# Attention scores: the two banks' products with the key's low half, 64 array rows each

## The chip, the cores and the metric

The kernel runs on one core of one Trainium2 chip. The metric is the device time of one execution in microseconds. The core has a matrix engine (TensorE, PE in the profile; its weight loads are listed as PEld), three engines for elementwise work (VectorE or DVE, ScalarE or ACT, GpSimd or POOL), and a synchronisation engine (SyncE, SP) that mostly issues DMA transfers. Each engine runs its own instructions in order and waits for the others through semaphores. The array of the matrix engine has 128 rows, along which a product is summed, and 128 columns; a stationary operand ("weights") is loaded into it, and a moving operand of up to 512 columns streams past. Results go to PSUM, in banks of 512 fp32 values for each of 128 partitions.

## The reference

One layer of a hybrid encoder is computed for a prompt of 1024 tokens and a decode sample of 32 tokens. The part that matters is the attention of the prompt over 8 heads of 64 values. An indexer has chosen 256 keys for each query; the others are masked out:

```python
s = jnp.einsum('bthd,btkhd->bthk', q.astype(f32), kg) * (HEAD_DIM ** -0.5)
s = jnp.where(valid[:, :, None, :], s, -jnp.inf)
p = jax.nn.softmax(s, axis=-1)
return jnp.einsum('bthk,btkhd->bthd', p, vg)
```

Queries of one chunk of 64 tokens see the keys up to the end of their chunk, so a tile of 128 queries, number i of 0 to 7, needs the first 128 (i + 1) keys. The kernel computes the scores of all these keys and adds a mask.

## The kernel before

Most products are made in a reduced fp32 format (`F32R`), in which one operand is split into a high half H and a low half L = x - H, and several products are added up in PSUM to win back the lost digits. The large projections do it with three (`mm3`, lines 272 to 274).

**Scores.** A head has only 64 values, half the rows of the array. The kernel uses the other half for the low part of the query: for head e of a pair (e is 0 or 1), `X.qs[e]` is a tile of 128 partitions, with the query's high half in the partitions 64e to 64e + 63 and its low half in the other 64. The key is stored twice, in both halves of the partitions of `X.kH[e]` (high) and `X.kL[e]` (low). A single product of `qs` with `kH` so gives q_high k_high + q_low k_high, and one of `qs` with `kL` adds q_high k_low + q_low k_low. `Soft.products` (line 1410) does these two products for each PSUM bank (line 1420): tiles with up to 512 keys have one bank, larger ones two banks of 320, 384, 448 or 512 columns (i = 4, 5, 6, 7). The order is kH, kL for the first bank, then kH, kL for the second.

**Order of the work.** Attention runs over four pairs of heads, p = 0 to 3, and in each over both heads and eight query tiles; these items stand in one list (`seq`). The loop at line 1730 takes one step for each item k: the scores of item k on TensorE; its row maxima on DVE, which read the PSUM banks (line 1426); the output product of item k - 3 (line 1530); the transposes of item k - 2 (line 1513), whose results ACT and DVE copy (1515, 1516); the exponentials of item k on ACT (line 1433), and normalisations (1440, 1442). Between these, `run(...)` deals in pieces of the large projections (the stream `Z`, `pz` in the profile), written out by hand so that TensorE has other work while the elementwise engines turn one tile's scores into weights. The pair p = 3 goes through its query tiles as i = 6, 7, 4, 5, 2, 3, 0, 1, the others from 0 to 7. An item of another kind (`Sample`, once in each pair) handles the 32 decode queries with plain fp32 operands; its transposes (line 1476) have only 64 rows, and one of its products (line 1485, tile `vts`) only 32.

`begin()` (line 1448) runs once for each pair, ahead of the scores of its first item; it loads the gate `Y[0]` over the DMA queue of SP. That queue also carries the weights of the projections (`raw`, line 251) and the heads' keys (`kd`, line 1305).

Of the kernel before, what the change touches and what calls it, by code (L numbers as in the profile page):

```python
# [8 lines left out]
F32R = mybir.dt.float32r  # L9
# [7 lines left out]
T, TS, D = 1024, 32, 1024  # L17
# [14 lines left out]
SQ, HF, SM, GD, GH, NP, BL, HB, GL = 1, 4, 3, (1, 1, 0), 1, (0, 0, 2, 2), 1, 1, 0  # L32
# [5 lines left out]
NP, HP = (0, 2), 100  # L38
# [25 lines left out]
def body(nc, tc, I, O, dbg=None):  # L64
# [3 lines left out]
    te, ve, se, ge, sp = nc.tensor, nc.vector, nc.scalar, nc.gpsimd, nc.sync  # L68

    def f32(ap):  # L70
        return ap.bitcast(F32)
# [21 lines left out]
    def ps_x(tag, bufs, w=512):  # L93
        t = phase[1].tile([128, w], F32, tag=tag, bufs=bufs, name="ps" + tag)
        return t
# [1068 lines left out]
    mb = {i: mbpool.tile([128, 128 * (i + 1)], BF16, name=f"mb{i}") for i in range(8)}  # L1164
# [46 lines left out]
    for k in range(9):  # L1211
# [4 lines left out]
        o = (k % 4) * 72  # L1216
# [10 lines left out]
    for j in range(4):  # L1227
# [3 lines left out]
        for i in range(2, 9):  # L1231
            t0, m, k0, nk = (128 * i - B0[1], 128, 0, 128 * (i + 1)) if i < 8 else (T - B0[1], 32, 1024, 544)
            for e in range(2):
# [5 lines left out]
                for a in range(nb):  # L1239
                    c = slice(k0 + a * w_, k0 + (a + 1) * w_)  # L1240
# [166 lines left out]

    class Soft:

        def products(self, m, nk, mask, lhsT, rhs, np_=0):  # L1410
            self.m, self.nk, self.mask, self.np_ = m, nk, mask, np_
            self.P = at2.tile([128, 1024], F32, name="Sm", bufs=SM)
            self.S = []
            w_ = nk // (1 + (nk > 512))
            for a in range(0, nk, w_):
                c = slice(a, a + w_)
                S = ps_x("s", 3)[:m, 0:c.stop - a]
                self.S.append((c, S))
                for t, r in enumerate(rhs):
                    te.matmul(S, lhsT, r[:, c], start=t == 0, stop=t == len(rhs) - 1)  # L1420

        def maxima(self):
            m = self.m
# [20 lines left out]
    def attention(p, X):  # L1444

        Y = {}

        def begin():
            if p < 3:
                Y[0] = stg.tile([128, NT], F32, name="ya", tag="stg")  # L1450
                sp.dma_start(Y[0], zaD[p])
            else:
                Y[0] = f32(ap_.tile([128, T], F32R, name="qs1", bufs=2))
                Y[1] = at2.tile([128, TS], F32, name="ys", bufs=1)
                sp.dma_start(Y[0], zaD[p][:, 0:T])
                sp.dma_start(Y[1], zaD[p][:, T:NT])
# [8 lines left out]
        class Sample(Soft):  # L1465
            e, i = -1, 4

            def scores(self):
                self.products(64, 544, mb8, X.qsm.rearrange("p e q -> p (e q)"), (X.kall,))
# [23 lines left out]
        class Rows(Soft):  # L1493
# [2 lines left out]

            def scores(self):
                e, i = self.e, self.i
                self.products(128, 128 * (i + 1), mb[i], X.qs[e][:, 128 * i:128 * i + 128], (X.kH[e], X.kL[e]),
                              NP[i % 2])  # L1500

            def turn(self):
                i, ii, P = self.i, self.ii, self.P
# [43 lines left out]
        if SF[p] == 2:  # L1547
            items.append(Sample())
        return items, begin, lambda: sp.dma_start(yaD[p], Y[0])


# [38 lines left out]
    X = Heads(0, ge, se)  # L1590
# [123 lines left out]
    at2 = stT.enter_context(tc.tile_pool(name="at2", bufs=1, side="right", reuse_waits="tile"))  # L1714
# [15 lines left out]
    for k in range(len(seq) + 3):  # L1730
        it = at(k)
        if k in first:
            p, begin = first[k]
# [169 lines left out]
    for rows in ((0, 1, 2), (8,), (3,), (4,), (5,), (6,), (LAST,)):  # L1903
        xts = {}
        for hcol in range(2):
            for i in rows:
# [6 lines left out]
                for b_, c in enumerate(cols):  # L1913
                    ps = products(i, n, hcol, c)
                    finish(i, n, hcol, c, ps, xt, hcol + b_)
                    if i == LAST:
                        hc = slice(512 * hcol + c.start, 512 * hcol + c.stop)
                        ve.tensor_tensor(xt[:n, hc], xt[:n, hc], gf[:n, hc], op=ALU.mult)
                    if len(cols) == 2 and b_ == 0:
                        ve.tensor_scalar(ss2[:n, 0, i:i + 1], ss2[:n, 0, i:i + 1], ss2[:n, 1, i:i + 1], None,  # L1920
                                         op0=ALU.add)
# [53 lines left out]
```

## Time and profile before

| what | value |
|---|---|
| median of 3 runs | 988.62 us (987.72 to 989.31) |
| the profiled execution, device time | 988.34 us |
| the same, span from first to last instruction | 986.6 us |
| granted TensorE clock, mean | 0.997 of full |
| DVE busy | 749.8 us (76%) |
| ACT busy | 527.7 us (53%) |
| POOL busy | 217.4 us (22%) |

The attention loop takes the stretch from about 576 to 831 us of the span. "Busy" of TensorE counts each product from its start to the modelled end of its passage through the array, and these overlap from one product to the next; how long a product really holds the engine is read from the distance between the starts of two neighbours. In the profile's rows a form such as `64*128 64x64` stands for an instruction on 64 rows and 128 columns of the array with an output of 64 x 64 (rows as the profile gives them; fp32 and the reduced format are both printed as f32).

### The profile page before, as it was taken

Reading aid. Unit: us, or ns where it says so; the run is one execution under the profiler, and the core shown is the slowest. Engines: PE = TensorE matmul, PEld = TensorE weight load, DVE = VectorE, ACT = ScalarE, POOL = GpSimd, SP = SyncE. Lnnn points to the kernel's source line nnn. Section 1 sums busy time; section 2 is a strip of 40 time slices with the busy share of each in tenths; the row PEclk is TensorE's granted clock in tenths of the full one; section 3 lists DMA queues with packets and bytes.
Section 4 is the critical chain, followed back from the end, with each engine's and each line's share of the span. In section 5 each row is a group of like instructions: output and inputs, shape, how many; then the busy total and the mean of one; then the engine's idle time right before and its main releaser. Section 6 shows DMA issues by size and latency. Waiting matters only on the chain.

```text
span 986.6 us, 16723 instructions
## 1 busy us (share of the span) xinstructions
PE 955.0 (97%) x5996; PEld 894.7 (91%) x5996; DVE 749.8 (76%) x1749; ACT 527.7 (53%) x1133; POOL 217.4 (22%) x363
## 2 busy tenths in 40 slices
PE   5999999999999999999999999999999999999997
PEld 4799999999999899999999999999999988998786
DVE  6779889991875868889998977777578786885543
ACT  6552233423655656867998356766576555343211
POOL 5002400000000021333323832234122212430000
PEclk9999999999999999999999999999999999999999
DMA  9922524447283221324223440241359203662311
GB/s 324 295 82 87 155 86 125 123 125 268 88 274 114 71 91 51 123 70 126 88 94 103 131 132 23 87 125 39 104 164 323 77 22 113 197 208 83 118 66 63
DMA packets 131312, 124.24 MB, mean 126 GB/s; under 512 B 20385, under 2 KB 109941, under 8 KB 131229
## 3 DMA queue, kind: packets, MB, share of 16 engines
q1 hardware_dynamic: 130288, 122.62, 39.9%
q8 instruction: 47, 0.77, 0.3%
q10 hardware_dynamic: 780, 0.52, 0.2%
q14 instruction: 37, 0.30, 0.1%
q0 software_dynamic: 160, 0.03, 0.0%
HBM read 87.74 MB, written 34.83 MB: 124 GB/s over the span
## 4 chain that ended last, share of the span: by engine, by line
PE 73%; DVE 10%; ACT 9%; issue 4%; DMA 2%; POOL 0%; SPq 0%; POOLq 0%; ACTq 0%; DVEq 0%
PE pz L272 12%; PE pz L273 12%; PE pz L274 12%; ACT junkb L1583 6%; PE pspo L1530 4%; PE pss L1420 4%; PE pt L1513 3%; PE psm L1946 3%; PE psm L1944 3%; PE psm L1945 3%; DVE junk L1585 2%; PE pss L1241 2%; PE pss L1242 2%; PE psm L273 1%; PE psm L274 1%
## 5 line engine op out<-in xcount | busy, mean ns | idle before, releaser
L272 PE MATMUL pz<-hH,wh 128*128 128x384 f32 (+4 forms) x760 | 258.3, 340 | 1.7 <-ACT zf L1334 1.7
L274 PE MATMUL pz<-hH,wl 128*128 128x384 f32 (+4 forms) x760 | 249.8, 329 | 0.4 <-DVE wl L265 0.4
L273 PE MATMUL pz<-hL,wh 128*128 128x384 f32 (+4 forms) x760 | 249.9, 329 | 0.0
L265 POOL TENSOR_TENSOR wl<-raw,wh 128x256 fp32r<-128x256 f32 (+1 forms) x172 | 122.7, 744 | 141.6 <-ACT wh L260 140.8
L272 PEld LDWEIGHTS pz<-hH,wh 128*128 128x128 f32 (+1 forms) x760 | 142.6, 188 | 6.9 <-ACT zf L1334 1.9
L273 PEld LDWEIGHTS pz<-hL,wh 128*128 128x128 f32 (+1 forms) x760 | 141.8, 187 | 2.0
L274 PEld LDWEIGHTS pz<-hH,wl 128*128 128x128 f32 (+1 forms) x760 | 141.6, 186 | 1.9 <-DVE wl L265 0.6
L1583 ACT ACTIVATE junkb<-sco,thr 128x768 bf16<-128x768 f32 (+3 forms) x128 | 96.8, 756 | 28.4 <-DVE thr L1665 18.1
L1585 DVE TENSOR_SCALAR_CACHE_REDUCE junk<-sco,thr 128x1024 bf16<-128x1024 f32 (+2 forms) x96 | 105.4, 1098 | 2.2
L272 PE MATMUL pss<-hH,wh 128*128 128x256 f32 (+1 forms) x272 | 84.9, 312 | 2.2 <-ACT tg L732 1.9
L273 PE MATMUL pss<-hL,wh 128*128 128x256 f32 (+1 forms) x272 | 84.1, 309 | 0.1
L274 PE MATMUL pss<-hH,wl 128*128 128x256 f32 (+1 forms) x272 | 83.9, 309 | 0.0
L264 POOL CAST wh<-raw 128x256 fp32r<-128x256 f32 x80 | 41.4, 559 | 181.2 <-PE pz L273 179.6
L1515 ACT CAST PH<-pt 128x512 fp32r<-128x512 f32 (+2 forms) x96 | 43.0, 482 | 34.7 <-PE pt L1513 34.3
L1249 DVE SCALAR_TENSOR_TENSOR sco<-rl,wi,sco 128x384 f32<-128x384 f32 (+6 forms) x49 | 45.5, 936 | 18.1 <-ACT rl L1244 17.1
L1516 DVE TENSOR_TENSOR PL<-pt,PH 128x512 fp32r<-128x512 f32 (+2 forms) x96 | 50.4, 552 | 11.6 <-ACT PH L1515 11.0
L272 PEld LDWEIGHTS pss<-hH,wh 128*128 128x128 f32 x272 | 51.5, 189 | 6.3 <-POOL wh L264 2.5
L1244 ACT ACTIVATE rl<-pss 128x384 f32<-128x384 f32 (+6 forms) x56 | 41.3, 740 | 29.3 <-PE pss L1242 24.1
L1433 ACT ACTIVATE Sm<-Sm,mx 128x128 f32<-128x128 f32 (+8 forms) x68 | 52.6, 774 | 1.3 <-DVE mx L1426 1.3
L1946 PE MATMUL psm<-o,mL 128*128 128x512 f32 (+1 forms) x136 | 52.0, 382 | 0.0
L1944 PE MATMUL psm<-o,mH 128*128 128x512 f32 (+1 forms) x136 | 51.7, 381 | 0.0
L1945 PE MATMUL psm<-o,mH 128*128 128x512 f32 (+1 forms) x136 | 51.6, 379 | 0.0
(415 smaller groups left out, 2164.0 us busy)
## 6 DMA issues: line engine op xcount, KB each, us to landing
raw<-in_w_in SPq DMA_DIRECT2D x42, 512.0 KB
thD<-tg SPq DMA_DIRECT2D x16, 528.0 KB
wm<-in_w_mod SPq DMA_DIRECT2D x16, 512.0 KB
m<-thD SPq DMA_DIRECT2D x8, 528.0 KB
tgl<-thD SPq DMA_DIRECT2D x8, 528.0 KB
xr<-in_x_prompt SPq DMA_DIRECT2D x8, 512.0 KB
rraw<-in_w_mod SPq DMA_DIRECT2D x4, 1024.0 KB
kd<-kd SPq DMA_DIRECT2D x32, 128.0 KB
```

Source lines behind the costliest of these rows:

```text
L265: leng.tensor_sub(wl[:, c], raw[:, c], f32(wh[:, c]))
L272: te.matmul(ps, wh, xh, start=first, stop=False)
L273: te.matmul(ps, wh, xl, start=False, stop=False)
L274: te.matmul(ps, wl, xh, start=False, stop=last)
L1249: ve.scalar_tensor_tensor(sco[i][:m, :nk], rl[:m, :nk], w, sco[i][:m, :nk], op0=ALU.mult, op1=ALU.add)
L1433: se.activation(P, P, AF.Exp, scale=-1.0, bias=self.mx, accum_out=self.rs)
L1516: ve.tensor_sub(PL[:, b0:b1_, oc], src, f32(PH[:, b0:b1_, oc]))
L1583: se.activation(junkb[:m, :nk], x[:m], AF.Sign, bias=t, accum_out=cnt[:m, k:k + 1])
L1585: ve.tensor_scalar(junk[:m, :nk], x[:m], t, None, op0=ALU.is_lt, op1=ALU.add, accum_out=cnt[:m, k:k + 1])
L1944: te.matmul(ps, mh, wh, start=first, stop=False)
L1945: te.matmul(ps, mh, wl, start=False, stop=False)
L1946: te.matmul(ps, ml, wh, start=False, stop=last)
```

## The change

For query tiles with more than 640 keys (i = 5, 6, 7) the products with `kL` are made differently; of pair 3, head 0, only i = 5 is treated so. Both banks first get their product with `kH`, as before on all 128 rows. Then follow two products that use 64 rows each: the first bank takes the query's high half from `qs` and the half of `kL` in the same partitions; the second bank takes a copy of the query's high half in the other 64 partitions (`qd`) and the half of `kL` that lies there. The two stand on different rows of the array and write different banks. The term q_low k_low is left out for these tiles. The copies `qd` are made for the columns 640 to 1023 by two DMA transfers in `begin()`, with one buffer for all four pairs.

```diff
-        def products(self, m, nk, mask, lhsT, rhs, np_=0):
+        def products(self, m, nk, mask, lhsT, rhs, np_=0, pair=None):
...
-                for t, r in enumerate(rhs):
-                    te.matmul(S, lhsT, r[:, c], start=t == 0, stop=t == len(rhs) - 1)
+                for t, r in enumerate(rhs[:1] if pair else rhs):
+                    te.matmul(S, lhsT, r[:, c], start=t == 0, stop=not pair and t == len(rhs) - 1)
+            if pair:
+                for (c, S), (q_, r) in zip(self.S, pair):
+                    te.matmul(S, q_, rhs[1][r, c], start=False, stop=True)
...
         def begin():
+            X.qd = at2.tile([128, 384], F32R, name="qd", bufs=1)
+            for e in range(2):
+                r, o = slice(64 * e, 64 * e + 64), slice(64 - 64 * e, 128 - 64 * e)
+                sp.dma_start(f32(X.qd[o]), f32(X.qs[e][r, 640:T]))
...
                 e, i = self.e, self.i
-                self.products(128, 128 * (i + 1), mb[i], X.qs[e][:, 128 * i:128 * i + 128], (X.kH[e], X.kL[e]),
-                              NP[i % 2])
+                t, pair = slice(128 * i, 128 * i + 128), None
+                if i > 4 and not (p == 3 and e == 0 and i > 5):
+                    r, o = slice(64 * e, 64 * e + 64), slice(64 - 64 * e, 128 - 64 * e)
+                    pair = ((X.qs[e][r, t], r), (X.qd[o, 128 * i - 640:128 * i - 512], o))
+                self.products(128, 128 * (i + 1), mb[i], X.qs[e][:, t], (X.kH[e], X.kL[e]), NP[i % 2], pair)
```

On TensorE the order changes only inside the scores of these tiles, in 22 places. This is the difference at the first of them (pair 0, head 0, i = 5), with the transposes of another item ahead (`Sm` holds the softmax weights, `pss` is a bank of scores, a name's number counts its buffers, and a shape is that of the output):

```order
 L272 MATMUL pz<-hH_551,wh 128x416
 L273 MATMUL pz<-hL_835,wh 128x416
 L274 MATMUL pz<-hH_551,wl 128x416
-L1420 MATMUL pss<-kH_4818,qs_4601 128x384
-L1420 MATMUL pss<-kL_4819,qs_4601 128x384
-L1420 MATMUL pss<-kH_4818,qs_4601 128x384
-L1420 MATMUL pss<-kL_4819,qs_4601 128x384
+L1420 MATMUL pss<-kH_4818,qs_4601 128x384 x2
+L1423 MATMUL pss<-kL_4819,qs_4601 128x384
+L1423 MATMUL pss<-kL_4819,qd 128x384
```

The two products with `kH` now stand together, and the two with `kL` follow as a pair; four products remain four, and a projection product on 128 rows (`pz`) comes right after them as before.

On SP the queue gets two transfers for each pair of heads. This is the place where pair 0 begins (`mb` is the mask of the decode queries, `ys` a gate, `kd` keys, `raw` weights of the projections, `out_v` an output):

```order
 L1291 DMA out_v_p<-tm 128x8x128
-L1706 DMA mb_3336<-mb_3336 32x544
-L1456 DMA ys<-zaD_250 128x32
+L1716 DMA mb_3336<-mb_3336 32x544
+L1455 DMA qd<-qs_4601 64x384
+L1455 DMA qd<-qs_4602 64x384
+L1305 DMA kd<-kd_6235 64x512
+L1292 DMA out_v_s<-tm 32x128
+L1305 DMA kd<-kd_6235 64x512
+L251 DMA raw<-in_w_in 128x8x128
+L1463 DMA ys<-zaD_250 128x32
+L251 DMA raw<-in_w_in 128x8x128
```

The copies `qd` stand ahead of keys and weights that were issued earlier in the row, and the gate `ys` moves behind them. DVE, ACT and POOL have the same instructions in the same order as before.

## The prediction, made before the changed kernel was run

> **What bounds the kernel now.** I read the head of the page first, then the busy times of the attention stretch, then the waits there, and last the starts of single products. The first two rows are of the page, the third is of the view of busy times by stretch (length; then busy time and number of instructions of PE, PEld, DVE, ACT, POOL; the clock last but two); the others are of the view of waits in that stretch (total us, times, longest).
>
> ```profile
> span 986.6 us, 16723 instructions
> PE 955.0 (97%) x5996; PEld 894.7 (91%) x5996; DVE 749.8 (76%) x1749; ACT 527.7 (53%) x1133; POOL 217.4 (22%) x363
> 576.00:831.00 255.00, 250.79 (x1717) 237.44 (x1716) 190.29 (x555) 162.05 (x374) 70.12 (x107) 1.00 0.32 103
> PEld pt L1513 <- ACT Sm L1440: 3.3, 6, 0.9
> PEld pspo L1530 <- DVE PL L1516: 1.4, 3, 0.8
> PEld pspo L1485 <- ACT PS L1478: 0.9, 1, 0.9
> DVE Sm L1426 <- PE pss L1420: 3.8, 7, 1.2
> ```
>
> In the 255 us of attention TensorE is busy 250.8 us, DVE 190.3, ACT 162.1. TensorE's waits there for the softmax (ACT, line 1440) and for copies and halves (1516, 1478) come to 3.3 + 1.4 + 0.9 = 5.6 us. So what TensorE spends more or less in a score tile reaches the end nearly in full; DVE waits for scores only 7 times, so most maxima start when DVE is free, not when the scores are there.
>
> **What a pass costs and what is saved.** Rows are starts and lengths of single products on TensorE: the score tiles i = 5, 6 and 7 of pair 0, head 0, from the first product with kH to the projection product behind the fourth.
>
> ```profile
> 592.65 0.34 PE L1420 MATMUL pss<-kH,qs 128*128 128x384 f32 x1
> 593.34 0.35 PE L272 MATMUL pz<-hH,wh 128*128 128x416 f32 x1
> ...
> 595.40 0.36 PE L1420 MATMUL pss<-kH,qs 128*128 128x448 f32 x1
> 596.22 0.28 PE L272 MATMUL pz<-hH,wh 128*128 128x256 f32 x1
> ...
> 600.42 0.39 PE L1420 MATMUL pss<-kH,qs 128*128 128x512 f32 x1
> 601.33 0.34 PE L272 MATMUL pz<-hH,wh 128*128 128x384 f32 x1
> ```
>
> Four passes take 0.69, 0.82 and 0.91 us, so one takes 0.17, 0.205 and 0.23 us: the length in a row (0.34) is latency, and the weights of the next product load under the running one. If two products of 64 rows run side by side, one pass in four goes. The change touches 8 tiles with i = 5 and 7 each with i = 6 and 7 (22 places in the order): 8 x 0.17 + 7 x 0.205 + 7 x 0.23 = **4.4 us saved**.
>
> **What is added: going to 64 rows and back.** The trace has places where TensorE leaves the full array for fewer rows and returns. Around 65.5 us one transpose of 32 rows stands alone between projection products; at 705.8 us the five transposes of a decode item with 64 rows stand between such products.
>
> ```profile
> 65.19 0.28 PE L273 MATMUL pz<-hL,wh 128*128 128x256 f32 x1
> 65.30 0.28 PE L274 MATMUL pz<-hH,wl 128*128 128x256 f32 x1
> 65.51 0.24 PE L547 MATMUL pt<-idf,dl 32*128 32x32 f32 x1
> 65.69 0.38 PE L272 MATMUL pz<-hH,wh 128*128 128x256 f32 x1
> 65.91 0.28 PE L273 MATMUL pz<-hL,wh 128*128 128x256 f32 x1
> ...
> 705.58 0.33 PE L274 MATMUL pz<-hH,wl 128*128 128x384 f32 x1
> 705.84 0.52 PE L1476 MATMUL pt<-idf,Sm 64*128 64x64 f32 x5
> 706.29 0.45 PE L272 MATMUL pz<-hH,wh 128*128 128x416 f32 x1
> 706.58 0.35 PE L273 MATMUL pz<-hL,wh 128*128 128x416 f32 x1
> 706.77 0.35 PE L274 MATMUL pz<-hH,wl 128*128 128x416 f32 x1
> ```
>
> The weight loads have rows of their own in the views by line (min/median/max in ns); those of the short transpose and of a score product:
>
> ```profile
> L547 PEld LDWEIGHTS pt<-idf,dl x1: 134/134/134, 65.5 to 65.5; 32*128 32x128 f32 x1
> L1420 PEld LDWEIGHTS pss<-kH,qs x72: 187/188/190, 580.0 to 822.1; 128*128 128x128 f32 x72
> ```
>
> A pass of 256 columns takes 0.11 us (65.19 to 65.30). At 65.30 it is 0.21 us to the next start: 0.10 more, in which nothing starts although no other engine is waited for. The first product back on 128 rows (65.69) takes 0.22 instead of 0.11: its weights could not be loaded under the one before, and a load listed with 0.19 us costs 0.11 when nothing hides it. The transpose's own load is listed with 0.13, so I estimate 0.05 for it; from its start to the next product it is 0.18, less 0.05 and 0.02 for its 32 columns, so 0.11 is empty again. At 705.58 the same: 0.26 instead of 0.17 going in, 0.29 instead of 0.19 (706.58 to 706.77) after coming back. From 705.58 to 706.58 there are 1.00 us, less the passes 0.17 and 0.19 is 0.64 for five transposes and both turns; with 0.03 us of streaming each (64 columns at 0.17 us for 384) 0.49 is left, with 0.06 each 0.34.
>
> For a pair I add: 0.09 empty going in, 0.10 for its own weights, which nothing hides (the 0.11 of a product behind such a gap; the load of these weights is that of a 128-column operand, not the shorter one of a transpose), 0.10 empty going out, 0.11 for the weights of the projection product behind: **0.40 us**. It could be 0.34 (the transposes' own case) or 0.50 (if the second half's weights load behind the first's). For 22 places: 8.8 us, between 7.5 and 11.0.
>
> The Trainium skill, "TensorEngine Tiling (Array Packing)", Key Properties, says that a change of the tiling mode drains TensorE, whatever tile is used. By that rule the pair pays both turns and the tiles lose time, and the rows above agree. By the following rows, where products on 32 and on 64 array columns alternate, a change of the tile's size need not cost anything, and only the 4.4 us saved would be left.
>
> ```profile
> 918.13 0.40 PE L1885 MATMUL psm<-o,mS 128*64 128x512 f32 x1
> 918.37 0.39 PE L1884 MATMUL psm<-o,mS 128*32 128x512 f32 x1
> 918.60 0.39 PE L1885 MATMUL psm<-o,mS 128*64 128x512 f32 x1
> ```
>
> They follow each other at 0.23 to 0.24 us, the price of a plain pass of 512 columns, so there no turn costs anything. These are products in the reduced format, as the pair is; no product of this format on 64 rows is in the trace. I side with the rows of fewer array rows, since rows are what the pair divides, and keep the others as a rival.
>
> **Do two tiles run side by side?** The trace shows it for columns, not for rows.
>
> ```profile
> 36.46 1.06 PE L295 MATMUL pmrow<-wm,scP 128*32 128x512 f32 x8
> 37.46 0.44 PE L272 MATMUL pss<-hH,wh 128*128 128x384 f32 x1
> ...
> 631.29 1.13 PE L1420 MATMUL pss<-kall,qsm 128*64 128x272 f32 x4
> 632.36 0.46 PE L272 MATMUL pz<-hH,wh 128*128 128x416 f32 x1
> ```
>
> Four fp32 records of 272 columns on one tile take 1.07 us, about 1 ns a column; eight records of 512 columns on four column tiles take 1.00 us where one after the other they would take 8 x 0.5 = 4. So tiles at different places of the array overlap, four deep. For two row tiles I take the same, with their weights loaded at the same time. No run shown here has row tiles side by side, so the serial case stays as a rival.
>
> **The rest.** The added transfers are eight, each of 64 rows of 1.5 KB. Their nearest row is a pair of key transfers (64 x 512):
>
> ```profile
> 581.77 1.10 SPq L1305 DMA_DIRECT2D kd<-kd  x2
> 583.59 15.24 SPq L251 DMA_DIRECT2D raw<-in_w_in  x2
> SPq L251 <- ACT wh L260: 49.2, 6, 12.5
> ```
>
> Two cost SP 1.1 us of issue and push keys and weights back by that; the weight loads wait for their buffer anyway (49.2 us in six waits, and the second load at 583.59 is issued some 15 us after the first), so I cost them at nothing. The first use of qd comes five items behind begin() (three in pair 3), and an item takes 255 / 68 = 3.75 us, so over 10 us pass and no product waits for it; without that cover a place would cost 1 us or two. A transfer of a later pair must wait until the last product has read qd, which precedes it on TensorE at once.
>
> DVE gets the first bank's scores later: they were complete after two passes, now after three and the 0.2 us of going in, that is 0.4 us later. The maxima have 0.4 us less slack in 22 of 64 tiles; TensorE's six waits for the softmax could grow by as much, at most 2.4 us. Against that the elementwise engines gain 4 us over 255 in which TensorE is slower, and some of the 5.6 us of waits will shrink. I take zero, between -1.5 and +1.5.
>
> **The sum**, against the profiled execution (988.34 us, of which 986.6 are span; 0.03% under the median 988.62): 8.8 - 4.4 = **+4.4 us, 992.7 us**. With 0.34 a place and -1.5 it is +1.6 (989.9), with 0.50 and +1.5 it is +8.1 (996.4); most likely 990.5 to 995.
>
> **Rivals.**
> - *No turns, side by side (faster).* Products of the reduced format go to 64 rows without emptying the array, as those at 918 us go between 32 and 64 columns. Then only the saving stays: 988.34 - 4.4 = 983.9 us. It decides as soon as a turn and its loads cost less than a pass, 0.17 to 0.23 us for both turns. Against it: both places in the trace with fewer rows show the gaps. 12%.
> - *Turns, but one after the other.* Two 64-row products queue up as 128-row ones do; the pair costs two passes and the turns: 988.34 + 8.8 = 997.1 us. Against it: the four column tiles at 36 us. 10%.
> - *Neither: it does not do what it says.* The array treats 64 rows as a full product with half of its rows idle, so nothing drains and nothing overlaps; four passes stay four: 988.3 us. For it: a narrow product at 918 us costs a full pass and no turn. 9%.
>
> **How the numbers follow.** The forecast has 69%. The range leaves out the first rival and little more: from 987.9, with the neutral one in, to 997.5, past the serial one; it holds about 8 in 10. A measurement of this kernel can tell about 0.2%, 2 us, from no change. Faster by more: the first rival, 0.12. Within: the neutral rival 0.09 and the low end of the forecast, 0.05, together 0.14. Slower by more: the forecast's other 64% and the serial rival, 0.74.
>
> **What would show it.** In the changed profile the two products of line 1423 should start within some 0.02 us of each other, about 0.26 to 0.32 us after the second product with kH, and the projection product behind should start a pass and 0.2 us after them and take 0.1 us more than its neighbours. From the first product of line 1420 to the second projection product the tile should grow by 0.40 minus a pass: 0.23, 0.20, 0.17 us. Starts a full pass apart mean the serial case, no gaps mean the first or third rival. Waits of line 1423 for the transfers, or longer waits of line 1513 for ACT, would show the parts costed at nothing. The prediction falls if the turns cost under 0.23 us together or if TensorE's waits absorb more than 2 us.

## The result: 4.5 us slower

| | before | after |
|---|---|---|
| median of 5 runs | 988.62 us (987.71 to 990.16) | 993.15 us (992.61 to 995.95) |
| span of the profiled execution | 986.6 us | 992.3 us |

The ratio is 1.0051, with a 95% interval of 1.0033 to 1.0069, that is 3.3 to 6.8 us. The forecast was 992.7 us. The profiled executions (988.34 and 994.09 us) lie 0.3 us under the one median and 0.9 us over the other, so their spans are 5.7 us apart and not 4.5.

### The profile page after: what moved, and what is told of

It is laid out like the page before. It is cut to its first block, busy times and chain, and to the rows that moved or that the text cites. A ratio compares the mean times of both kernels' runs of the same rounds, so it can differ in the third digit from the quotient of the medians.

```text
span 992.3 us, 16737 instructions
## 1 busy us (share of the span) xinstructions
PE 958.3 (97%) x5996; PEld 887.5 (89%) x5996; DVE 751.4 (76%) x1749; ACT 527.4 (53%) x1133; POOL 216.5 (22%) x363
## 4 chain that ended last, share of the span: by engine, by line
PE 71%; DVE 11%; ACT 9%; issue 4%; DMA 3%; POOL 1%; SPq 0%; ACTq 0%; POOLq 0%; DVEq 0%
PE pz L272 12%; PE pz L273 11%; PE pz L274 11%; ACT junkb L1593 5%; PE pspo L1540 4%; PE pt L1523 3%; PE psm L1956 3%; PE psm L1954 3%; PE pss L1420 3%; PE psm L1955 3%; DVE junk L1595 2%; PE pss L1241 2%; PE pss L1242 2%; PE psm L273 1%; PE psm L272 1%
```

## The profile after

The head of the page, the stretch of attention (260 us now, to its later end) and TensorE's and DVE's waits in it, in the same views as before:

```profile
span 992.3 us, 16737 instructions
PE 958.3 (97%) x5996; PEld 887.5 (89%) x5996; DVE 751.4 (76%) x1749; ACT 527.4 (53%) x1133; POOL 216.5 (22%) x363
576.00:836.00 260.00, 255.77 (x1722) 232.71 (x1721) 192.03 (x558) 162.01 (x374) 69.68 (x107) 1.00 0.34 104
PEld pss L1423 <- issue: 6.7, 22, 0.4
PEld pz L272 <- issue: 6.1, 25, 0.4
PEld pt L1523 <- ACT Sm L1443: 2.4, 5, 0.9
DVE Sm L1429 <- PE pss L1423: 1.9, 5, 0.6
PEld pt L1523 <- ACT Sm L1436: 1.2, 1, 1.2
```

and one row of the waits before:

```profile
PEld pz L272 <- issue: 1.6, 4, 0.4
```

TensorE stays busy nearly all the time, and the work of DVE and ACT is what it was. Two rows have the releaser "issue". The first is new: the weight loads of the pairs, 22 times, stood still while the profile shows no engine or transfer that they waited for. The second, weight loads of projection products (line 272) such as those behind the pairs, grew from 4 waits to 25. I read both as the array being emptied; the profile itself shows only that no weight load runs there. The times cannot be added to the loss as they stand, since "idle" here means that no weight load was running, and the array still streams for part of it.

The same tiles as before, i = 5 and i = 7 of pair 0, head 0, by the starts of single products:

```profile
593.76 0.51 PE L1420 MATMUL pss<-kH,qs 128*128 128x384 f32 x2
594.21 0.44 PE L1423 MATMUL pss<-kL,qs 64*128 64x384 f32 x1
594.21 0.44 PE L1423 MATMUL pss<-kL,qd 64*128 64x384 f32 x1
594.59 0.46 PE L272 MATMUL pz<-hH,wh 128*128 128x416 f32 x1
594.88 0.35 PE L273 MATMUL pz<-hL,wh 128*128 128x416 f32 x1
595.07 0.35 PE L274 MATMUL pz<-hH,wl 128*128 128x416 f32 x1
...
601.75 0.63 PE L1420 MATMUL pss<-kH,qs 128*128 128x512 f32 x2
602.31 0.49 PE L1423 MATMUL pss<-kL,qs 64*128 64x512 f32 x1
602.32 0.49 PE L1423 MATMUL pss<-kL,qd 64*128 64x512 f32 x1
602.74 0.44 PE L272 MATMUL pz<-hH,wh 128*128 128x384 f32 x1
603.01 0.34 PE L273 MATMUL pz<-hL,wh 128*128 128x384 f32 x1
603.19 0.34 PE L274 MATMUL pz<-hH,wl 128*128 128x384 f32 x1
```

The weight loads of the first of these pairs:

```profile
594.21 0.18 PEld L1423 LDWEIGHTS pss<-kL,qs 64*128 64x128 f32 x1 [0.25 <-issue]
594.21 0.18 PEld L1423 LDWEIGHTS pss<-kL,qd 64*128 64x128 f32 x1
```

The two halves start together, their weights load at the same time, and the pair is over after one pass: they do run side by side. But two passes with kH of 512 columns and the way in take 0.56 us (601.75 to 602.31) where two passes are 0.46; the pair takes 0.43 to the next product (602.31 to 602.74), a pass and 0.20; and the first product behind takes 0.27 instead of 0.18. That is 0.10 + 0.20 + 0.09 = 0.39 us for the detour, against 0.23 saved. For i = 5 it is 0.45 - 0.34 = 0.11, then 0.38 - 0.17 = 0.21, then 0.29 - 0.19 = 0.10: 0.42, against 0.17. With the starts in ns the same sum is 0.38 to 0.41 us in each of the 22 pairs, 0.40 on average.

## Experiments

The theory is that going to 64 rows and back costs about 0.41 us of empty array and unhidden weight loads, whatever stands in the detour, and that a pair saves one pass. The rivals: the loss comes from the new order (DVE gets the first bank late); from the transfers; or the two halves do not overlap after all. The first four ran together on one chip, where before had a median of 989.24 us (19 runs).

**e1: the order alone**

```diff
...
-                sp.dma_start(f32(X.qd[o]), f32(X.qs[e][r, 640:T]))
...
-                    pair = ((X.qs[e][r, t], r), (X.qd[o, 128 * i - 640:128 * i - 512], o))
+                    pair = ((X.qs[e][:, t], slice(0, 128)), (X.qs[e][:, t], slice(0, 128)))
```

> The low products stay on all 128 rows and q_low k_low is computed again; only the order of the change is kept (both banks' products with kH, then both with kL), without the copies qd. If the loss is the price of going to 64 rows and back, it is gone: within 1 us of before (988.6 us). If it comes from the order, that is from DVE getting the first bank's scores later, the 4.5 us stay: about 993 us.

Measured: 990.22 us, ratio 1.0003 (0.999 to 1.0015). In its trace tile i = 7 takes the four passes of before:

```profile
602.21 0.61 PE L1420 MATMUL pss<-kH,qs 128*128 128x512 f32 x2
602.66 0.62 PE L1423 MATMUL pss<-kL,qs 128*128 128x512 f32 x2
603.11 0.34 PE L272 MATMUL pz<-hH,wh 128*128 128x384 f32 x1
603.29 0.34 PE L273 MATMUL pz<-hL,wh 128*128 128x384 f32 x1
```

From 602.21 to 603.11 are 0.90 us, and the product behind takes a plain 0.18. The order costs nothing that can be measured (the interval reaches from -1.0 to +1.5 us), so the loss lies in the 64 rows or in the copies. The first bank is complete one pass later here, not the 0.4 us later of the changed kernel, so this run tests about half of that delay.

**e2: both halves on the same rows**

```diff
-                    pair = ((X.qs[e][r, t], r), (X.qd[o, 128 * i - 640:128 * i - 512], o))
+                    pair = ((X.qs[e][r, t], r), (X.qs[e][r, t], r))
```

> Both 64-row products use the same half of the array (query's high half from qs, the same half of kL), so they cannot run side by side; the copies qd are still made but not read. If the turns cost 0.41 us a tile and side by side saves a pass, the saving of 8 x 0.16 + 7 x 0.19 + 7 x 0.21 = 4.1 us goes: about 997.2 us, second product of line 1423 starting a pass behind the first. If the two products of the changed kernel did not really overlap, the time stays at 993 us.

Measured: 999.12 us, ratio 1.0091 (1.0059 to 1.0122), so 5.8 to 12.1 us over before; expected were 8.6.

```profile
603.61 0.63 PE L1420 MATMUL pss<-kH,qs 128*128 128x512 f32 x2
604.17 0.73 PE L1423 MATMUL pss<-kL,qs 64*128 64x512 f32 x2
604.83 0.44 PE L272 MATMUL pz<-hH,wh 128*128 128x384 f32 x1
605.11 0.34 PE L273 MATMUL pz<-hL,wh 128*128 128x384 f32 x1
```

The pair now takes 0.66 us (604.17 to 604.83) instead of 0.43: a pass of 0.23 more, the way in and out as in the changed kernel. Side by side is real and worth a pass; it is just worth less than the detour. The copies qd are made here too, so this run says nothing of their price.

**e3: two detours a tile**

```diff
-            if pair:
-                for (c, S), (q_, r) in zip(self.S, pair):
-                    te.matmul(S, q_, rhs[1][r, c], start=False, stop=True)
+                if pair:
+                    q_, r = pair[len(self.S) - 1]
+                    te.matmul(S, q_, rhs[1][r, c], start=False, stop=True)
```

> The order of before (kH, kL, kH, kL), each low product on 64 rows, so every tile goes to 64 rows and back twice and nothing runs side by side. If a detour costs 0.41 us whatever stands in it: 22 x 2 x 0.41 = 18 us over before, about 1006.6 us. If detours cost less than a pass (the loss of the change lies in order, transfers or waits), under 993 us.

Measured: 1005.38 us, ratio 1.0152 (1.0128 to 1.0176), so 12.7 to 17.4 us over before; the span of the profiled execution is 1004.5, 17.9 over that of before, of which 1.3 lie ahead of the first score product.

```profile
602.88 0.40 PE L1420 MATMUL pss<-kH,qs 128*128 128x512 f32 x1
603.20 0.49 PE L1423 MATMUL pss<-kL,qs 64*128 64x512 f32 x1
603.63 0.50 PE L1420 MATMUL pss<-kH,qs 128*128 128x512 f32 x1
604.06 0.49 PE L1423 MATMUL pss<-kL,qd 64*128 64x512 f32 x1
604.48 0.44 PE L272 MATMUL pz<-hH,wh 128*128 128x384 f32 x1
604.76 0.34 PE L273 MATMUL pz<-hL,wh 128*128 128x384 f32 x1
```

The tile takes 1.60 us (602.88 to 604.48) instead of 0.91, and the product behind 0.28 instead of 0.17: 0.80 us for two detours, 0.40 each. The detour costs the same when it saves nothing and when it comes twice. 22 x 0.80 = 17.6 us is what TensorE pays, and from the first score product to the end the trace is 16.6 us longer than before. So about 1 us of it was taken up on the way; by what was not settled. The expected 18 us lie just outside the interval.

**e4: all four products on 64 rows**

```diff
-                for t, r in enumerate(rhs[:1] if pair else rhs):
+                for t, r in enumerate([] if pair else rhs):
...
-            if pair:
+            for h in range(2 if pair else 0):
                 for (c, S), (q_, r) in zip(self.S, pair):
-                    te.matmul(S, q_, rhs[1][r, c], start=False, stop=True)
+                    te.matmul(S, q_, rhs[h][r, c], start=h == 0, stop=h == 1)
```

> Leaves out q_low k_high as well as q_low k_low for the 22 tiles: all four products take 64 rows, two and two side by side, in one detour. Two passes are saved instead of one. With 0.41 us for a detour: 8 x (0.41 - 0.345) + 7 x (0.41 - 0.41) + 7 x (0.41 - 0.455) = +0.2 us, about 988.8 us. If the weights of the second two products are not loaded under the first two, 0.1 us more a tile: 991 us. If detours cost nothing: 988.6 - 8.8 = 979.8 us.

Measured: 990.14 us, ratio 1.0004 (0.9988 to 1.002).

```profile
601.59 0.34 PE L274 MATMUL pz<-hH,wl 128*128 128x384 f32 x1
601.86 0.50 PE L1423 MATMUL pss<-kH,qs 64*128 64x512 f32 x1
601.86 0.49 PE L1423 MATMUL pss<-kH,qd 64*128 64x512 f32 x1
602.20 0.39 PE L1423 MATMUL pss<-kL,qs 64*128 64x512 f32 x1
602.20 0.39 PE L1423 MATMUL pss<-kL,qd 64*128 64x512 f32 x1
602.52 0.44 PE L272 MATMUL pz<-hH,wh 128*128 128x384 f32 x1
602.80 0.33 PE L273 MATMUL pz<-hL,wh 128*128 128x384 f32 x1
```

One detour that saves two passes comes out even, as reckoned: the way in is 0.27 - 0.17 = 0.10, the first pair takes 0.34 (a pass and its weights, which nothing hides), the second 0.32 (a pass and the way out), the product behind 0.28 instead of 0.17. That gives the four parts of the detour one by one: 0.10, 0.11, 0.09 and 0.11. The weights of the second pair were loaded under the first: their loads start at 601.97, 0.11 us after the first pair. This also bounds the copies, which are made here as in the changed kernel: the sum without them came to +0.2 us, and the interval reaches from -1.2 to +2.0 us, so they cost 2 us at the most. In the trace the stretch from the first score product to the end is 0.1 us longer than before, and no row of the waits has line 1423 waiting for a transfer.

**e5 and e6: the same price where the kernel before pays it**

If a detour costs 0.3 to 0.4 us anywhere, the kernel before has some to give up, in the decode items: fp32 products on 64 columns (the scores of `qsm`) and on 32 rows (`vts`), and transposes on 64 rows. e5 pads the first two with zeros to the full array:

```diff
-                self.vts = ap_.tile([32, 128], F32, name="vts", bufs=3)
-                ge.tensor_copy(self.vts, self.vt[:32, 8])
+                self.vts = ap_.tile([128, 128], F32, name="vts", bufs=3)
+                ge.memset(self.vts, 0.0)
+                ge.tensor_copy(self.vts[:32], self.vt[:32, 8])
...
-                self.qsm = ap_.tile([128, 2, TS], F32, name="qsm", bufs=2)
+                self.qsm = ap_.tile([128, 4, TS], F32, name="qsm", bufs=2)
...
-                S = ps_x("s", 3)[:m, 0:c.stop - a]
-                self.S.append((c, S))
+                S = ps_x("s", 3)[:lhsT.shape[1], 0:c.stop - a]
+                self.S.append((c, S[:m]))
...
+                ge.memset(self.PS[:, 4], 0.0)
...
-                    te.matmul(po[:, 0:64], X.cvt[:, k] if k < 4 else X.vts, self.PS[:n, k], start=k == 0, stop=k == 4)
+                    te.matmul(po[:, 0:64], X.cvt[:, k] if k < 4 else X.vts, self.PS[:, k], start=k == 0, stop=k == 4)
```

> The kernel of before, with two detours of the decode items taken out: the product with 32 rows (vts) and the scores on 64 columns are padded with zeros to 128 rows and 128 columns; same results. If a detour costs its price wherever it stands, 4 x 0.35 us (vts: 0.80 us from the last product ahead to the second behind, less 0.45 for the passes) and 4 x 0.33 us (scores: 1.62 less 1.29) are saved: 2.7 us under before. If the loss of the change belongs to its own tiles alone (their order, copies or PSUM use), nothing is saved.

e6 does the same with the transposes:

```diff
+                ge.memset(self.P[64:128, 0:544], 0.0)
...
-                    te.transpose(pt[:n, k * 64:k * 64 + 64], P[:64, k * 128:k * 128 + n], idf[:64, :64])
+                    te.transpose(pt[:n, k % 4 * 128:k % 4 * 128 + 128], P[:, k * 128:k * 128 + n], idf)
...
```

> As e5, and the five transposes of a decode item on 128 rows too (rows 64 to 127 zeroed by POOL, results in two PSUM banks). Another detour goes, 4 x 0.34 us, but each transpose streams 128 columns instead of 64, 4 x 5 x 0.05 us: 0.4 us under e5, 3.1 us under before. If POOL's zeroing comes late, TensorE waits for it and the gain is lost.

Measured, against 990.11 us for before on the same chip (23 runs): e5 988.54 us, ratio 0.9982 (0.9971 to 0.9994); e6 988.53 us, ratio 0.9988 (0.9976 to 1.0). In the trace of before, the scores of the first decode item with the products around them, and its product with 32 rows:

```profile
631.03 0.34 PE L274 MATMUL pz<-hH,wl 128*128 128x384 f32 x1
632.65 0.35 PE L273 MATMUL pz<-hL,wh 128*128 128x416 f32 x1
...
645.66 0.43 PE L1485 MATMUL pspo<-PS,vts 32*128 32x64 f32 x2
646.25 0.28 PE L273 MATMUL pz<-hL,wh 128*128 128x256 f32 x1
```

In e5's trace the scores and the last product of the first decode item read:

```profile
635.38 0.34 PE L274 MATMUL pz<-hH,wl 128*128 128x384 f32 x1
635.56 1.08 PE L1421 MATMUL pss<-kall,qsm 128*128 128x272 f32 x4
...
636.66 0.35 PE L273 MATMUL pz<-hL,wh 128*128 128x416 f32 x1
...
649.54 0.39 PE L1487 MATMUL pspo<-PS,vts 128*128 128x64 f32 x2
...
649.94 0.28 PE L273 MATMUL pz<-hL,wh 128*128 128x256 f32 x1
```

and in e6's the transposes of the second:

```profile
707.01 0.34 PE L274 MATMUL pz<-hH,wl 128*128 128x384 f32 x1
707.19 0.71 PE L1478 MATMUL pt<-idf,Sm 128*128 128x128 f32 x5
...
707.93 0.35 PE L273 MATMUL pz<-hL,wh 128*128 128x416 f32 x1
```

The scores take 1.28 us from the product ahead to the second one behind (635.38 to 636.66); before it was 1.62 (631.03 to 632.65), with the same products around (the scores themselves stand in the prediction's rows at 631.29). From the start of `vts` to the second product behind it is 0.40 us (649.54 to 649.94), before 0.59 (645.66 to 646.25); the way in is 0.09 shorter too, so `vts` saves 0.28 where 0.35 was expected. The transposes take 0.92 us (707.01 to 707.93) instead of 1.00. So the price is not one of the score tiles: padding the products to the whole array, with as many columns to stream, is cheaper than a turn. e5 is faster than before by about 1.6 us; its interval, 0.6 to 2.9 us, does not reach zero and holds both the expected 2.7 and the 4 x 0.34 + 4 x 0.28 = 2.5 us of the rows. e6 adds 4 x 0.08 = 0.3 us on TensorE, less than these runs can tell, and is not shown to be better than e5.

**All kernels from the first score product to the end.** Ahead of attention the profiled executions differ by up to 4 us, although in the changed kernel and in e1 to e4 TensorE's instructions there are those of before: the first score product starts at 580.1 us of the span before, at 581.2 in the changed kernel, at up to 582.9 in e1 to e4 and at 584.4 in e5. So I take the rest of the span from there, one profiled execution each:

| kernel | from there to the end | against before | expected |
|---|---|---|---|
| before | 406.5 us | | |
| changed | 411.1 us | +4.6 | +4.4 |
| e1 | 407.0 us | +0.4 | 0 (within 1) |
| e2 | 415.2 us | +8.7 | +8.6 |
| e3 | 423.1 us | +16.6 | +18 |
| e4 | 406.6 us | +0.1 | +0.2 |
| e5 | 404.2 us | -2.3 | -2.7 |
| e6 | 403.8 us | -2.8 | -3.1 |

For e5 and e6 this leaves out what their zeroing on POOL may cost ahead of attention.

## Why the prediction was right

- **What bounds.** TensorE, as said: what it spent more in the tiles came out at the end.
- **The pass saved.** 0.17, 0.205 and 0.23 us by the rows of before; e2, which takes the overlap away, lost 0.23 for i = 7. This is shown.
- **The detour.** Put at 0.40 us from two transposes and the price of an unhidden weight load; the pairs of the changed kernel paid 0.39 and 0.42 in the rows above, 0.40 on average, and e3 0.40 apiece. The parts were right too, not only their sum: 0.09, 0.10, 0.10 and 0.11 forecast, 0.10, 0.11, 0.09 and 0.11 in e4. The high end of 0.50 did not occur, since the weights of both halves load at the same time. The low end of 0.34, read off the transposes of a decode item, is near what other products of these items pay (0.28 and 0.34 in e5), but not what the pairs pay.
- **The rule and the rows against it.** The Trainium skill, "TensorEngine Tiling (Array Packing)", Key Properties, has a change of mode drain TensorE; for the 64 rows of the reduced format the 22 pairs agree with it, at 0.10 us empty going in. That this gap is the emptying, and not some other cost of the turn, no run separates. The products on 32 and 64 columns at 918 us, which paid nothing, were no model for rows.
- **The rest at nothing.** e1 shows it for the order and for half of DVE's later start. In the changed kernel DVE waits 5 times, 1.9 us, for the pairs, besides 3.7 us for the products of line 1420 (3.8 before, when all scores were made there). TensorE's transposes wait about as long for ACT as before: 2.4 us for line 1443 (3.3 before, line 1440), but 1.2 us in one new wait for line 1436. The 22 tiles add 4.4 us by the starts of their products, and from the first score product to the end it is 4.6, so all the rest is worth about 0.2 us. For the copies e4 leaves 2 us at most by the runs and next to nothing by its trace; they were not tried alone.
- **The sum.** 8.8 - 4.4 = 4.4 us forecast, 4.5 us measured in the medians. Of the 5.7 us between the two profiled spans 1.1 lie ahead of the first score product. Most of that is one wait of TensorE for ACT (line 1334) near 567 us, 2.8 us instead of 1.9; in e4, whose program is the same up to there, it takes 1.9 us, so it is not the work of the change.
- **The rivals.** Turns free, halves one after the other, or neither: the starts of line 1423, the gaps, and e2 exclude all three. That the middle of the forecast came within 0.5 us is in part luck: its own bounds for the rest were 1.5 us either way.

## What to carry to other kernels

A product with half the rows pays only if the detour to fewer rows saves more than about 0.4 us of streaming, which here is nearly two passes of 512 columns; one pair of passes in a detour loses, two come out even (e4). Elsewhere the price differs somewhat: 0.28 and 0.34 us in the decode items. So collect the narrow products in one place (by this sum; more than two pairs in a detour were not tried), or pad them with zeros to the full array when there are few and the padding adds no columns to stream, as in e5. The price can be read beforehand, here to about 0.1 us, from any place in a trace where a form with fewer rows stands between full ones: compare the distance between starts there with the plain pass of the same width.

## What was not expected of the hardware

Narrow columns behave in two ways. The reduced-format products on 32 and 64 columns at 918 us (0.23 us a pass) pay no turn, while the plain fp32 scores on 64 columns did: padding them to 128 columns took 0.34 us off each decode item. The rows at 918 us follow one another; the trace of before also has reduced-format products on 32 columns between full ones, and they pay nothing going in or out:

```profile
316.96 0.35 PE L274 MATMUL pz<-hH,wl 128*128 128x416 f32 x1
317.15 0.29 PE L1241 MATMUL pss<-kiH,qis 128*32 128x272 f32 x1
...
317.65 0.35 PE L272 MATMUL pz<-hH,wh 128*128 128x416 f32 x1
317.84 0.35 PE L273 MATMUL pz<-hL,wh 128*128 128x416 f32 x1
```

The way in takes 0.19 us, a plain pass of 416 columns, and so does the product behind. Why the fp32 scores differ from these was not settled.

Weights for the same 64 rows also load under a running product of those rows: in e4 the second pair started 0.34 us after the first, a pass and one unhidden load, not two.
